# The gate sums of the last pair of experts held in their own PSUM bank across a conditional part, with the silu behind it

## The chip, the core and the metric

The kernel runs on one core of a Trainium2 chip. The time is the device time of one execution in microseconds (us); the median of three runs of the kernel before is 784.7 us. The engines have streams of their own and meet at semaphores: TensorE (PE, its weight loads PEld), VectorE (DVE), ScalarE (ACT), GpSimd (POOL) and the queue that issues most DMAs (SP).

## What is computed

A trunk of two layers over 256 tokens of width 1024. Each layer has a mixer and then a mixture of experts; the change is in the experts alone.

```python
def grouped_moe(h, router_w, router_bias, w_gate, w_up, w_down):
    ...                                  # router: two of 16 experts for each token
    y = jnp.zeros_like(hf)
    for e in range(N_EXPERTS):           # 16 experts, 1024 -> 512 -> 1024
        act = jax.nn.silu(hf @ w_gate[e]) * (hf @ w_up[e])
        y = y + combine[:, e:e + 1].astype(hf.dtype) * (act @ w_down[e])
    return y.reshape(bsz, s_len, d)

def reference(...):
    for l in range(DEPTH):               # DEPTH = 2
        ...
        x = x + g1 * mix
        h = rmsnorm(x, norm_ffn[l]) * (1.0 + sc2) + sh2
        x = x + g2 * grouped_moe(h, router_w, router_bias, moe_w_gate[l], moe_w_up[l], moe_w_down[l])
    return rmsnorm(x, final_norm)
```

## The kernel before

The experts are taken in eight pairs, `pr` 0 to 7. For a pair, up to 64 tokens (`CAP`) of each of its two experts are gathered into `xg` (once for two pairs), multiplied with the gate weights (`up(..., "g")`, tile `g`, 32 matmuls in the trace) and with the up weights (tile `u`, 32), and `act` is silu(g) times u. `actT` transposes it, `down` multiplies with the down weights (tile `dn`, 32), `evicted` and `high_low` scale the result and split it in two parts (`ys`), and `scatter` adds it to the accumulators `acc`, which hold their four banks for the whole stage. The work of a pair overlaps that of the next: while pair `pr` has its gate sums made, the result of `pr - 1` or `pr - 2` is being scaled and scattered.

Weights come in pieces of 1 MB, 12 for a pair, into a ring of 16 buffers; SP issues them in the order in which they are used, each as soon as its buffer was read for the last time. In layer 0 the last down piece of pair 7 is issued by POOL (line 1518, `following`), behind a one-element copy (line 1590, tile `cs`) that reads the first down piece of that pair and so starts when that one has landed.

Short-lived sums take turns in three PSUM banks (`bank`, tag `ps`, `bufs=3`): a request gets the bank that was given out longest ago and waits until what was in it has been read. `bankx` is one more bank, for transposes.

If an expert has more than 64 tokens, `rest` (lines 1396 to 1434) does the pairs' remaining tokens. It is code that is skipped when no count exceeds 64; with these inputs the branch to its end is taken on every engine, in both layers. `rest` is written in the middle of pair 7: behind the gate sums and the scatter of pair 5 (lines 1509, 1510), ahead of `down` of pair 6 and the up sums of pair 7. What is waited for across the skipped part works by counts: each engine that jumps over it adds, at the place it jumps to, what its skipped instructions would have added to its own semaphore (`EVENT_SEMAPHORE` on line 1398), and an instruction behind the branch that needs a bank which the skipped part would have used waits for that count. The engines take the branch independently, each when its own stream gets there.

Line 1512, ahead of `rest`, takes the silu of pair 7's gate sums from their bank to SBUF (`sg`), since `rest` would use the three banks:

```python
            if pr == 7:
                for h in range(2):
                    scattered(h)
                sg = live.tile([128, 512], F32, tag="sq", name=f"sg{l}_7", bufs=2)
                S.activation(sg, gb_, AF.Silu)
                ...
                rest(quad, top=top, ...)
                ...
                late = scales(6, down(6, iter(w6), at), old)
```

## Time and profile before

| | us |
|---|---|
| median of three runs (784.68 to 785.6) | 784.7 |
| the profiled execution | 782.88 |
| its span, first to last instruction | 781.2 |
| TensorE matmuls busy | 717.0 |
| VectorE busy | 314.9 |
| ScalarE busy | 235.0 |

The trace is of one execution; what it does not cover is 1.7 us around the span. Times in the trace count from the start of the span. The experts of layer 0 run from about 200 to 420 us, those of layer 1 from about 553 us to the end.

In a timeline row the first number is the start, the second how long the row's instructions took together, and the bracket the idle time of the engine ahead of it and what ended that. An engine's name with a q is its sequencer: it branches, waits and issues DMAs while the engine itself is idle or still works. `ACTq L1398` is ScalarE's sequencer at the branch of `rest`.

### The profile page before, as it was taken

The numbers are of one execution on the slowest core, as the hardware profiler recorded it, in microseconds if no ns is written. First come the engines' busy times: TensorE is split into PE (matmuls) and PEld (weight loads), VectorE is DVE, ScalarE is ACT, GpSimd is POOL, SyncE is SP. The second block draws the span as 40 slices with busy tenths as digits, with TensorE's granted clock in tenths as the row PEclk, the third lists the DMA queues.
The fourth block names the chain that finished last, engine by engine and source line by source line (L and its number), as shares of the span: only waits on it lengthen the run. The fifth ranks groups of instructions, "written<-read, shape, count | busy, mean of one in ns | idle before, by whom it ended". The sixth has DMA issues, their size and how long they took to land. (4 is left out here: it accounts for less than half of the span.)

```text
span 781.2 us, 10574 instructions
## 1 busy us (share of the span) xinstructions
PE 717.0 (92%) x4121; PEld 393.3 (50%) x4121; DVE 314.9 (40%) x567; ACT 235.0 (30%) x441; POOL 120.8 (15%) x168
## 2 busy tenths in 40 slices
PE   6798878998999999999798999999899999999985
PEld 4398643676434445343233777579434334434323
DVE  4459979566213113121114745454513123213214
ACT  3457667544102001110112535552402001001012
POOL 2357658022000000000004500010300000000000
PEclk9999999998999999999999899999999999999999
DMA  9999769964999999999999999496799999999993
GB/s 358 385 372 420 312 231 362 374 227 159 350 411 409 410 409 409 409 409 409 409 404 371 396 412 349 173 404 251 291 393 410 409 409 409 409 409 409 410 403 108
DMA packets 74712, 282.45 MB, mean 362 GB/s; under 512 B 5194, under 2 KB 6438, under 8 KB 69530
## 3 DMA queue, kind: packets, MB, share of 16 engines
q1 hardware_dynamic: 73122, 278.68, 90.7%
q0 software_dynamic: 1344, 2.64, 1.0%
q8 instruction: 34, 0.56, 0.3%
q10 hardware_dynamic: 184, 0.34, 0.1%
q14 instruction: 28, 0.23, 0.1%
HBM read 280.59 MB, written 1.05 MB: 361 GB/s over the span
## 5 line engine op out<-in xcount | busy, mean ns | idle before, releaser
L1267 PE MATMUL g<-w,xg 128*64 128x512 f32 x512 | 114.8, 596 | 2.8 <-DMA w<-in_moe_w_gate_dram 1.8
L1267 PE MATMUL u<-w,xg 128*64 128x512 f32 x496 | 110.7, 594 | 2.5 <-DMA w<-in_moe_w_up_dram 2.5
L1300 PE MATMUL dn<-w,at 128*64 128x512 f32 x448 | 101.7, 604 | 7.7 <-ACTq L1398 6.5
L1279 DVE TENSOR_TENSOR act<-sg,u 128x512 f32<-128x512 f32 (+1 forms) x18 | 11.1, 628 | 153.7 <-PE u L1267 153.7
L1267 PEld LDWEIGHTS u<-w,xg 128*64 128x64 f32 x496 | 34.5, 137 | 72.5 <-issue 64.1
L1267 PEld LDWEIGHTS g<-w,xg 128*64 128x64 f32 x512 | 34.9, 137 | 69.4 <-issue 60.9
L429 PE MATMUL pj<-hT,g 128*128 128x256 f32 x480 | 61.7, 286 | 5.7 <-DVE g L56 4.5
L1300 PEld LDWEIGHTS dn<-w,at 128*64 128x64 f32 x448 | 31.2, 138 | 70.4 <-issue 56.8
L56 DVE TENSOR_TENSOR g<-wi,g 128x512 fp32r<-128x512 f32 x72 | 57.0, 801 | 23.7 <-ACT g L55 22.4
L429 PEld LDWEIGHTS pj<-hT,g 128*128 128x128 f32 x480 | 58.1, 189 | 9.8 <-DVE g L56 6.6
L459 PE MATMUL po<-cat,g 128*128 128x256 f32 x372 | 52.9, 296 | 3.9 <-ACT gsr L1021 1.7
L55 ACT ACTIVATE g<-wi 128x512 fp32r<-128x512 f32 x72 | 44.5, 626 | 38.0 <-PE pj L429 20.6
L424 PE MATMUL pj<-g,hT 128*128 128x512 f32 x192 | 51.2, 419 | 5.1 <-ACT hT L350 3.1
L190 PE MATMUL ada<-ad,cond 128*32 128x512 f32 x384 | 50.1, 630 | 4.9 <-DMA ad<-in_ada_w_dram 4.9
L459 PEld LDWEIGHTS po<-cat,g 128*128 128x128 f32 x372 | 48.1, 201 | 9.3 <-issue 2.7
L424 PEld LDWEIGHTS pj<-g,hT 128*128 128x128 f32 x192 | 36.7, 198 | 19.1 <-DVE g L56 4.2
L565 DVE SCALAR_TENSOR_TENSOR yc<-yp,epar,yc 128x256 f32<-128x256 f32 x56 | 41.4, 754 | 2.3 <-POOL yc L580 1.7
L580 POOL TENSOR_TENSOR yc<-yc,cv 128x256 f32<-128x256 f32 x45 | 39.2, 872 | 19.7 <-ACT cv L579 12.0
L1332 ACT ACTIVATE ys<-y 128x512 fp32r<-128x512 f32 x28 | 16.9, 625 | 66.8 <-DVE y L1322 62.0
L1290 DVE COPY at<-at 128x512 f32<-128x512 f32 x14 | 9.7, 692 | 67.2 <-PE at L1289 67.2
L1326 ACT ACTIVATE y<-dn,cw 128x512 f32<-128x512 f32 x7 | 4.8, 687 | 104.1 <-PE dn L1300 104.1
L1275 ACT ACTIVATE sg<-g 128x512 f32<-128x512 f32 x14 | 8.4, 597 | 89.3 <-PE g L1267 89.3
(381 smaller groups left out, 859.6 us busy)
## 6 DMA issues: line engine op xcount, KB each, us to landing
w<-in_moe_w_gate_dram SPq DMA_DIRECT2D x64, 1024.0 KB, 17.2
w<-in_moe_w_up_dram SPq DMA_DIRECT2D x62, 1024.0 KB, 18.3
w<-in_moe_w_down_dram SPq DMA_DIRECT2D x61, 1024.0 KB, 18.1
ad<-in_ada_w_dram SPq DMA_DIRECT2D x48, 1024.0 KB, 8.3
wi<-in_w_in_even_dram SPq DMA_DIRECT2D x20, 512.0 KB, 12.3
wi<-in_w_in_odd_dram SPq DMA_DIRECT2D x14, 512.0 KB, 12.5
wo<-in_w_out_even_dram SPq DMA_DIRECT2D x4, 1024.0 KB
wo<-in_w_out_odd_dram SPq DMA_DIRECT2D x4, 1024.0 KB, 18.7
```

The costliest lines, as they stand in the source:

```text
L55: S.activation(g[0], w, AF.Copy)
L56: (eng or V).tensor_tensor(g[1], w, g[0].bitcast(F32), op=OP.subtract)
L190: PE.matmul(acc[32 * j:32 * j + 32, :], lhsT=cond[:, k, :], rhs=w[:, k - (i if n == 2 else 2 * i), c0:c0 + 512], start=i == 0, stop=i == 4 ...
L424: PE.matmul(bs[t], lhsT=self.h[j][:, k, t * 128:(t + 1) * 128], rhs=g[i], start=k == 0 and p == 0, stop=k == 7 and p == 2)
L429: PE.matmul(bs[c // 2][:, (c % 2) * T:(c % 2 + 1) * T], lhsT=g[i][:, c * 128:(c + 1) * 128], rhs=self.h[j][:, k, :], start=k == 0 and c % ...
L459: PE.matmul(self.acc[kd // 2][:, (kd % 2) * T:(kd % 2 + 1) * T], lhsT=block(g[wi], kd % 4), rhs=cats[ci][:, k, :], start=start and kd % 2 ...
L565: V.scalar_tensor_tensor(yc[:, k], yp[:, k, j:j + T], epar[:, k, j:j + 1], yc[:, k], op0=OP.mult, op1=OP.add)
L580: G.tensor_tensor(y, y, p, op=OP.add)
L1267: PE.matmul(b[64 * e:64 * e + 64, :], lhsT=xg[:, k, o + 64 * e:o + 64 * e + 64], rhs=we[:, e, k % 2 * 512:k % 2 * 512 + 512], start=k == 0 ...
L1279: V.tensor_tensor(a[:, n], sg[:, n], ub[:, n], op=OP.mult)
L1300: PE.matmul(bs[h][64 * e:64 * e + 64, :], lhsT=at[k][:, 64 * e:64 * e + 64], rhs=r[:, e], start=k == 0, stop=k == 3)
L1332: S.activation(ys[:, 0, n], y[h], AF.Copy)
```

## The change

`bank` gets a turn counter. Two requests of three get one of two banks under the tag `ps`, the third the one bank under a tag of its own, `pq`. Requests made inside `rest` (`two=True`) use the two `ps` banks only and don't advance the counter. The counter is set to 1 at pair 6 of each layer, so that the gate sums of pair 7 fall on `pq`; they stay there across `rest`, and the silu is written behind it. Because the counter is set, requests later in the program may fall on another of the three banks than before.

```diff
-    def bank(name):
-        return psum.tile([128, 512], F32, tag="ps", name=name)
+    turn = [0]
+
+    def bank(name, two=False):
+        tag, bufs = ("ps", 2) if two or turn[0] % 3 < 2 else ("pq", 1)
+        turn[0] += not two
+        return psum.tile([128, 512], F32, tag=tag, name=name, bufs=bufs)
...
             def all(self, q, s=0):
                 self.onehot(q, s)
                 self.weighted(q)
-                self.gather(q, s)
+                self.gather(q, s, two=True)
...
-                                b = bank(f"o{l}_{pr}_{s}")
+                                b = bank(f"o{l}_{pr}_{s}", True)
...
-                                b = bank(f"o{l}_{pr}_{s}{h}")
+                                b = bank(f"o{l}_{pr}_{s}{h}", True)
...
             if pr == 6:
+                turn[0] = 1
...
                 for h in range(2):
                     scattered(h)
-                sg = live.tile([128, 512], F32, tag="sq", name=f"sg{l}_7", bufs=2)
-                S.activation(sg, gb_, AF.Silu)
 
                 w6, w, w7 = ([*ws] for ws in (weights(6, 8, 12), w, weights(7, 8, 12 if l else 11)))
                 rest(quad, top=top, spare=live.tile([128, 8 * T], F32, tag=("h", "xT")[l], name=f"spare{l}", bufs=(2, 1)[l])
                      .rearrange("p (i n) -> p i n", i=4))
                 if following:
                     w7.append(following(w7[0], lambda: weight(7, 11, eng=G)))
+
+                sg = live.tile([128, 512], F32, tag="sq", name=f"sg{l}_7", bufs=2)
+                S.activation(sg, gb_, AF.Silu)
                 late = scales(6, down(6, iter(w6), at), old)
```

(`gather` and `gathers` hand `two` on to `bank`.) No engine has an instruction more or less that works on data; line numbers behind `bank` are 5 to 7 higher after the change. Three places show what moved.

ScalarE in layer 0, before, at the end of the code ahead of the branch (`sg_6` and `sg_7` are the silus of pairs 6 and 7, `y_5` and `ys_5` the scaled and split result of pair 5, `COMPARE_AND_BRANCH` the branch of `rest`):

```order
L1275 ACTIVATE sg_6_0_2839<-g_6_0_2789 128x512 [waits DVE_49,PE_49]
L1326 ACTIVATE y_5_00_2885<-dn_5_00_2859,cw_2_2385 128x512 [waits DVE_49,PE_49]
L1332 ACTIVATE ys_5_0_2896<-y_5_00_2885 128x512 [waits Activation_49]
L1332 ACTIVATE ys_5_0_2896<-y_5_01_2894 128x512 [waits DVE_49]
L1512 ACTIVATE sg_7_2942<-g_7_0_2901 128x512 [waits PE_49]
L1398 COMPARE_AND_BRANCH
```

The same stretch after the change:

```order
L1280 ACTIVATE sg_6_0_2839<-g_6_0_2789 128x512 [waits DVE_49,PE_49]
L1331 ACTIVATE y_5_00_2885<-dn_5_00_2859,cw_2_2385 128x512 [waits DVE_49,PE_49]
L1337 ACTIVATE ys_5_0_2896<-y_5_00_2885 128x512 [waits Activation_49]
L1337 ACTIVATE ys_5_0_2896<-y_5_01_2894 128x512 [waits DVE_49]
L1403 COMPARE_AND_BRANCH
```

ScalarE behind the branch, after the change (the branch leads to the `UNCONDITIONAL_BRANCH` that waits; `y_6` and `ys_6` are the scaled and split result of pair 6):

```order
L1403 UNCONDITIONAL_BRANCH [waits Activation_49,Activation_sequencer_49]
L1525 ACTIVATE sg_7_7748<-g_7_0_2901 128x512 [waits PE_49]
L1331 ACTIVATE y_6_00_7768<-dn_6_00_7750,cw_3_2667 128x512 [waits DVE_49,PE_49,Activation_49]
L1337 ACTIVATE ys_6_0_7772<-y_6_00_7768 128x512 [waits Activation_49]
L1337 ACTIVATE ys_6_0_7772<-y_6_01_7770 128x512 [waits DVE_49]
```

The silu, which waits for TensorE's gate sums, went from ahead of ScalarE's branch to the first place behind it; nothing else on ScalarE moved, in either layer.

TensorE in layer 0 behind the branch, before (`dn_6` are the down sums of pair 6 with their four pieces of weights `w_6_8` to `w_6_11`, `u_7` the up sums of pair 7; rows without a wait between them are left out):

```order
L1398 UNCONDITIONAL_BRANCH [waits PE_49,PE_sequencer_49]
L1300 MATMUL dn_6_00_7750<-w_6_8_2944,at_6_2887 64x512 [waits DVE_49,DMAHW2_49,PE_49,Activation_49]
L1300 MATMUL dn_6_01_7751<-w_6_8_2944,at_6_2887 64x512 [waits DVE_49,Activation_49]
L1300 MATMUL dn_6_00_7750<-w_6_9_2946,at_6_2887 64x512 [waits DMAHW3_49]
L1300 MATMUL dn_6_00_7750<-w_6_11_2950,at_6_2887 64x512 [waits DMAHW5_49]
L1267 MATMUL u_7_0_7777<-w_7_4_2952,xg_3_2665 64x512 [waits DMAHW6_49]
```

and after:

```order
L1403 UNCONDITIONAL_BRANCH [waits PE_49,PE_sequencer_49]
L1305 MATMUL dn_6_00_7750<-w_6_8_2942,at_6_2887 64x512 [waits DVE_49,DMAHW2_49,PE_49,Activation_49]
L1305 MATMUL dn_6_01_7751<-w_6_8_2942,at_6_2887 64x512 [waits DVE_49,PE_49,Activation_49]
L1305 MATMUL dn_6_00_7750<-w_6_9_2944,at_6_2887 64x512 [waits DMAHW3_49]
L1305 MATMUL dn_6_00_7750<-w_6_11_2948,at_6_2887 64x512 [waits DMAHW5_49]
L1272 MATMUL u_7_0_7777<-w_7_4_2950,xg_3_2665 64x512 [waits DMAHW6_49,Activation_49]
```

The down sums still wait for a count of ScalarE that its jump adds; the up sums now wait for ScalarE too, for the silu that empties `pq`.

TensorE in the mixer of layer 1, before (four groups of pooling sums `py`, ahead of them the sums `alow`):

```order
L853 MATMUL alow<-hT_7970,walow 32x256 x8
L858 MATMUL py_8129<-ppt_8091,inpw 128x256 [waits DMASW1_49,Activation_49]
L858 MATMUL py_8134<-ppt_8097,inpw 128x256 [waits Activation_49]
L858 MATMUL py_8137<-ppt_8103,inpw 128x256 [waits DVE_49]
L858 MATMUL py_8140<-ppt_8109,inpw 128x256 [waits DVE_49]
L190 MATMUL ada_7900<-ad_8147,cond 32x512 [waits DMAHW3_49]
```

and after:

```order
L858 MATMUL alow<-hT_7970,walow 32x256 x8
L863 MATMUL py_8129<-ppt_8091,inpw 128x256 [waits DMASW1_49,Activation_49]
L863 MATMUL py_8134<-ppt_8097,inpw 128x256 [waits Activation_49]
L863 MATMUL py_8137<-ppt_8103,inpw 128x256 [waits DVE_49]
L863 MATMUL py_8140<-ppt_8109,inpw 128x256
L195 MATMUL ada_7900<-ad_8147,cond 32x512 [waits DMAHW3_49]
```

No row moved, but the banks were dealt out in another turn. Before, the third `py` waited until VectorE had read the first one's bank, and the fourth until VectorE had copied `alow` out of its bank; after, it is the third that gets the bank of `alow` and waits for that copy, and the fourth waits for nothing more.

## Rows read from the trace of the kernel before

**Rows 1.** Chain that ended last, first pieces: start, us, what

```profile
746.08 0.04 issue
746.12 7.09 PE dn L1300 x32
```

**Rows 2.** Timeline of layer 1 around the branch

```profile
735.27 0.64 ACT L1332 ACTIVATE ys<-y 128x512 fp32r<-128x512 f32 x1 [1.34 <-DVE y L1322]
...
740.79 2.14 PE L1356 MATMUL acc<-ys,pt 128*128 128x512 f32 x8
740.91 0.60 ACT L1512 ACTIVATE sg<-g 128x512 f32<-128x512 f32 x1 [5.01 <-PE g L1267]
...
746.12 7.09 PE L1300 MATMUL dn<-w,at 128*64 128x512 f32 x32 [3.19 <-ACTq L1398]
```

**Rows 3.** Sequencers at the branch, both layers: count, ns min/median/max, first and last start

```profile
L1398 DVEq EVENT_SEMAPHORE  x4: 21/21/21, 384.8 to 741.6; - x4
L1398 PEldq EVENT_SEMAPHORE  x4: 51/51/51, 388.9 to 743.1; - x4
L1398 ACTq EVENT_SEMAPHORE  x4: 17/17/17, 392.0 to 746.1; - x4
...
L1398 DVEq COMPARE_BRANCH  x2: 74/82/90, 379.1 to 735.9; - x2
L1398 PEldq COMPARE_BRANCH  x2: 355/371/387, 386.6 to 738.1; - x2
L1398 ACTq COMPARE_BRANCH  x2: 54/61/68, 386.7 to 740.9; - x2
```

**Rows 4.** TensorE's own waits of line 1300 behind the branch, layer 0

```profile
L1300 PEldq EVENT_SEMAPHORE  x2: 51/51/51, 389.2 to 389.3; - x2
```

**Rows 5.** The same waits in layer 1

```profile
L1300 PEldq EVENT_SEMAPHORE  x2: 51/51/51, 743.3 to 743.4; - x2
```

**Rows 6.** Timeline of layer 0 around the branch

```profile
378.45 0.63 ACT L1332 ACTIVATE ys<-y 128x512 fp32r<-128x512 f32 x1 [1.47 <-DVE y L1324]
...
386.60 2.21 PE L1350 MATMUL acc<-pt,ys 128*128 128x256 f32 x16
386.72 0.60 ACT L1512 ACTIVATE sg<-g 128x512 f32<-128x512 f32 x1 [7.64 <-PE g L1267]
...
392.09 8.78 PE L1300 MATMUL dn<-w,at 128*64 128x512 f32 x32 [3.28 <-ACTq L1398]
```

**Rows 7.** Timeline of layer 0, to the last down piece

```profile
409.23 0.19 POOL L1590 COPY cs<-w 128x1 f32<-128x1 f32 x1 [197.38 <-SPq L1398]
409.87 0.81 POOL L1251 DMA_DIRECT2D w<-in_moe_w_down_dram  x1 [0.46 <-issue]
...
416.82 1.94 PE L1300 MATMUL dn<-w,at_7arow 128*64 128x512 f32 x8 [0.48 <-DMA w<-in_moe_w_down_dram]
```

**Rows 8.** Stretches of TensorE: start:end, us, busy (x), granted clock, DMA share, GB/s

```profile
575.00:740.00 165.00, 165.00 (x820) 1.00 1.03 409
392.60:396.10 3.50, 3.50 (x12) 0.51 1.03 407
```

**Rows 9.** SP's last weight DMA in the timeline

```profile
757.90 1.24 SPq L1248 DMA_DIRECT2D w<-in_moe_w_down_dram  x1
```

**Rows 10.** The same DMA among the issues: KB, us to landing

```profile
w<-in_moe_w_down_dram SPq DMA_DIRECT2D x1, 256.0 KB, 8.8
```

**Rows 11.** TensorE's last matmuls of line 1300

```profile
L1300 PE MATMUL dn<-w,at_7arow x6: 379/379/379, 769.5 to 770.0; 128*64 128x256 f32 x6
```

**Rows 12.** Timeline of the pooling sums in the mixer of layer 1

```profile
451.44 1.92 PE L858 MATMUL py<-ppt,inpw 128*128 128x256 f32 x6 [0.47 <-ACT ppt L846]
452.18 0.42 DVE L862 COPY alowT<-alow 128x256 f32<-128x256 f32 x1 [0.63 <-PE py L858]
...
452.66 0.30 PEld L858 LDWEIGHTS py<-ppt,inpw 128*128 128x128 f32 x2 [0.49 <-DVE alowT L862]
453.29 0.16 PEld L190 LDWEIGHTS ada<-ad,cond 128*32 128x32 f32 x8 [0.33 <-issue]
```

## Prediction

> **What bounds the kernel now.** I read the chain that ended last first. It begins at 746.08 us, at the branch of `rest` in layer 1, and TensorE's down sums of pair 6 are its next piece [rows 1]: from there to the end everything follows on TensorE and then on the final scaling, so what starts those down sums sooner ends the kernel sooner. The timeline there shows TensorE idle for 3.19 us ahead of them, until ScalarE's sequencer at line 1398 let go [rows 2]; layer 0 has the same hole, 3.28 us [rows 6].

> The view of the sequencers tells why ScalarE is the last. Each engine branches when its stream gets there and reports from the other side later: VectorE branches at 379.1 and 735.9 and reports from 384.8 and 741.5 (the last of its four counts starts at 741.6), 5.6 us later; ScalarE branches at 386.7 and 740.9 and reports at 392.0 and 746.1, 5.2 to 5.3 us later [rows 3]. The branch itself takes ScalarE 54 to 68 ns, so the rest of the 5.2 us lies between it and the code behind it. ScalarE comes late because the silu stands ahead of its branch and waits for the gate sums: idle for 7.64 us in layer 0 and 5.01 in layer 1 [rows 2, 6]. TensorE's own reports start at 388.9 and about 743.0 (the second of the pair at 743.1) [rows 3], right as its scatter of pair 5 is done: 386.60 + 2.21 = 388.81 and 740.79 + 2.14 = 742.93 [rows 2, 6].

> **The change, part by part.** *The silu behind the branch.* It removes nothing and adds no work: two silus of 0.60 us [rows 2, 6] change place. ScalarE's last instruction ahead of the branch is now the split of pair 5's result, which starts at 378.45 and 735.27 [rows 2, 6]. Sequencers run ahead of their engines by one instruction here (the branch at 740.9 goes with a silu that starts at 740.91), so ScalarE branches at about 378.5 and 735.3. With its 5.3 us it reports at 383.8 and 740.6; with VectorE's 5.6 us, and branching only when the split has ended, at 384.7 and 741.5. Either is ahead of TensorE's own report.

> What is late next is TensorE itself: report, then its remaining waits for the first down sums, which start at 389.2 and 389.3 in layer 0 and at 743.3 and 743.4 in layer 1, 0.05 us each [rows 4, 5]. Counting from the last wait's start with its 0.05 and as much for the first weight load, the down sums can start at 389.4 and 743.5. Before they started at 392.09 and 746.12 [rows 2, 6]: 2.7 us sooner in layer 0, 2.6 in layer 1. VectorE's report, 1.4 us and more ahead of TensorE's, holds nothing up.

> *What the silu's new place could hold up.* Behind it on ScalarE stands the scaling of pair 6, which needs the down sums. The new wait is that of the up sums of pair 7 for the bank `pq`: the silu still starts when the gate sums are done, at 386.7 and 740.9, and is over 0.6 us later [rows 2, 6], while the up sums come 32 down matmuls, 7.09 us [rows 2], behind the branch. Cost nothing; if the silu's start were tied to ScalarE's report it would still be over by 742.1.

> *Layer 0, what becomes of 2.7 us.* Nothing, I think. The last down piece of pair 7 is issued by POOL at 409.87, behind a copy at 409.23 that waits for another piece's landing, and TensorE stands idle 0.48 us for it before it goes on at 416.82 [rows 7]. That issue hangs on transfers alone, so it stays where it is; TensorE comes up to 2.7 us sooner and waits that much longer. Bounds 0 to 2.7; I take 0, since the wait is there already.

> *Layer 1.* TensorE is busy for all of the 165 us from 575 to 740, at full clock, beside a DMA share of 1.03 [rows 8]. Behind it the weights must be there sooner. SP's last DMA is issued at 757.90 and lands 8.8 us later, at 766.7 [rows 9, 10]. Its four matmuls are the last of the six that start from 769.5 to 770.0 [rows 11], so they start at about 769.7; their waits may stand one pair of matmuls, 0.2 us, ahead. That leaves 2.8 us, 0.2 more than needed. So 2.6 us counts in full, at most 2.8.

> *The banks' new turn.* In the mixer of layer 1 the third `py` now waits for the copy of `alow`, which ends at 452.60. Before, only the fourth did; it starts its loads at 452.66, and the loads for `ada` follow at 453.29 [rows 12], 0.63 us on. After, the third starts where the fourth did, and the fourth and `ada` move back by the third's time: at least 0, if a later wait absorbs it, at most those 0.63 us. I take 0.4: in the 0.63 us are 0.33 us that the row calls issue [rows 12], part of which will overlap. TensorE is nearly always busy in this stretch, so I count it.

> *Sum.* The profiled execution is 782.88: 782.88 - 2.6 + 0.4 = 780.7. It stands 1.8 us below the median of the runs, 784.7; the same difference there gives 784.7 - 2.2 = **782.5 us**, 0.28% less. From both terms' ends: 784.7 - 2.8 = 781.9 to 784.7 - 2.6 + 0.6 = 782.7.

> [...]

> **The rivals.** *Serial jumps (slower).* VectorE and ScalarE now branch within 0.7 us of each other. If what the 5.2 us go for is served one engine at a time, ScalarE would begin when VectorE is through: in layer 1 at 741.5 + 5.3 = 746.8, after the 746.1 of before, 0.7 us lost; the hole is then 3.9 us, and after the 3.28 us of layer 0 the granted clock fell to 0.51 [rows 8], the lower of its two levels, and the same 32 matmuls took 8.78 instead of 7.09 us [rows 2, 6]: 1.7 more. With the 0.4 of the banks: 784.7 + 0.7 + 1.7 + 0.4 = 787.5. It decides from a jump of 10.2 us (746.1 - 735.9). Against it: in layer 1 VectorE's and TensorE's jumps ran together from 738.1 to 741.5, and VectorE's 5.6 us were the same in layer 0, where it jumped alone. Chance 4 in 100. [...]

> *The weights bind the end of layer 1.* TensorE and the transfers are nearly tied there, with 0.2 us left. In runs in which the last landing is 1 to 2.8 us later against TensorE's work, the gain shrinks by 0.8 to all of it: 783.3 to 785.1. For it: a DMA share of 1.03 over the whole stage. Against: the landing goes by issue times that the change does not touch, and a TensorE that is 0.4 us later at the start of the stage widens the room. Chance 15 in 100, at about 784.1.

> *More than the sum.* The hole of layer 1 is nearly as long as that of layer 0, and in the runs that were timed it may often cost the clock too, 1.7 us, which a hole of 0.5 us would not: 780.8, chance 10 in 100. Layer 0's 2.7 us could pass if the last piece came earlier: 779.8, 5 in 100.

> *It doesn't do what it says.* Something else that TensorE waits for comes at the same time as ScalarE's report and keeps the hole: 785.1. The rows name only ScalarE, twice. 4 in 100.

> **How the numbers follow.** The forecast, 782.5, has 62 in 100. The range 780.5 to 784.4 leaves out the serial jumps, the change without effect, layer 0's gain and the later part of the weights' case, some 20 in 100. A measurement of this kernel can tell about 0.2%, 1.6 us, from no change: faster means below 783.1. That holds for the forecast but for a few in 100 (0.6 us of banks and a little less gain), and for the two cases of more: 0.74. Slower means above 786.3: 0.04. The rest, 0.22, is the same.

> **What the profile would show.** Right: ScalarE's branches near 378.5 and 735.3, its reports before 385 and 742; the silu behind them, still at the end of the gate sums; TensorE's idle time ahead of the down sums of pair 6 about 0.6 us in both layers; in layer 0 more waits of TensorE for weights behind the branch and the last down piece again near 416.8; in layer 1 the chain shorter by 2.6 us with the last down matmuls close behind the last landing; the third `py` on `alowT`. Wrong: a ScalarE report later than TensorE's, waits for down weights at 764 to 768 us, or a layer 0 that ends more than 0.5 us away from where it does.

## The result and the profile after

Beside fresh runs of the kernel before, the changed kernel takes 780.34 us (median of 15 runs, 779.22 to 783.76) against 784.7 (median of 15, 782.52 to 787.36). The ratio is 0.9949, 95% interval 0.9933 to 0.9965: 4.0 us less, between 2.7 and 5.3. Forecast were 782.5 us and 2.2 us less. The direction was right; the median lies 0.16 us under the low end of the range, by the ratio (784.7 x 0.9949 = 780.7) just inside it, and the size is what the experiments are about.

The profiled execution takes 781.72 us, its span is 780.0 (before 781.2). What the prediction looked for is in its trace. First the chain that ended last, its first pieces (start, us, what), which answers to [rows 1]:

```profile
744.62 0.30 issue
744.92 7.09 PE dn L1305 x32
```

Layer 1 around the branch in the timeline, which answers to [rows 2]:

```profile
736.70 0.63 ACT L1337 ACTIVATE ys<-y 128x512 fp32r<-128x512 f32 x1 [1.34 <-DVE y L1327]
...
742.23 2.14 PE L1361 MATMUL acc<-ys,pt 128*128 128x512 f32 x8
742.35 0.60 ACT L1525 ACTIVATE sg<-g 128x512 f32<-128x512 f32 x1 [5.01 <-PE g L1272]
...
744.92 7.09 PE L1305 MATMUL dn<-w,at 128*64 128x512 f32 x32 [0.56 <-PEq L1403]
```

The silu still starts when the gate sums are done, but the down sums of pair 6 no longer wait for ScalarE's sequencer: they start 0.55 us behind the scatter's end (742.23 + 2.14 = 744.37), after 3.19 us before [rows 2], and what ends the rest of the hole is TensorE's own sequencer (PEq). The sequencers at the branch, now line 1403, in both layers (count, ns min/median/max, first and last start; answers to [rows 3]):

```profile
L1403 ACTq EVENT_SEMAPHORE  x4: 17/17/17, 385.5 to 742.0; - x4
L1403 DVEq EVENT_SEMAPHORE  x4: 21/21/21, 386.5 to 743.1; - x4
L1403 PEldq EVENT_SEMAPHORE  x4: 51/51/51, 390.6 to 744.6; - x4
L1403 POOLq COMPARE_BRANCH  x2: 54/54/54, 222.4 to 577.6; - x2
L1403 POOLq EVENT_SEMAPHORE  x2: 17/17/17, 222.6 to 577.8; - x2
L1403 ACTq COMPARE_BRANCH  x2: 54/61/68, 380.2 to 736.7; - x2
L1403 DVEq COMPARE_BRANCH  x2: 74/82/90, 380.8 to 737.4; - x2
```

ScalarE branches with the start of its last split (736.70) and reports 5.3 us later in layer 0 and 5.2 in layer 1 (the first of the pair at 741.9), VectorE 5.7 and 5.6 us after its own branch. Both are ahead of TensorE, whose reports come last. ScalarE's and VectorE's jumps now run side by side, 0.6 to 0.7 us apart, and each takes what it took alone: the rival of serial jumps is out.

Layer 0, to the end of its down sums, which answers to [rows 6, 7]:

```profile
388.31 2.20 PE L1355 MATMUL acc<-pt,ys 128*128 128x256 f32 x16
388.42 0.60 ACT L1525 ACTIVATE sg<-g 128x512 f32<-128x512 f32 x1 [7.62 <-PE g L1272]
...
391.14 5.37 PE L1305 MATMUL dn<-w,at 128*64 128x512 f32 x24 [0.63 <-PEq L1403]
...
396.95 1.94 PE L1305 MATMUL dn<-w,at 128*64 128x512 f32 x8 [0.44 <-DMA w<-in_moe_w_down_dram]
...
417.74 1.94 PE L1305 MATMUL dn<-w,at_7arow 128*64 128x512 f32 x8 [0.88 <-DMA w<-in_moe_w_down_dram]
```

The hole is as short as in layer 1, the clock does not fall (24 matmuls in 5.37 us, 0.22 each, at a granted clock of 1.00), and then TensorE waits for weights: already within pair 6's down sums, and 0.88 us for the last piece, 0.48 before [rows 7].

The mixer of layer 1, which answers to [rows 12]:

```profile
452.35 0.70 PE L863 MATMUL py<-ppt,inpw 128*128 128x256 f32 x2 [0.47 <-ACT ppt L851]
453.08 0.42 DVE L867 COPY alowT<-alow 128x256 f32<-128x256 f32 x1 [0.63 <-PE py L863]
...
453.56 1.13 PE L863 MATMUL py<-ppt,inpw 128*128 128x256 f32 x4 [0.52 <-DVE alowT L867]
454.62 1.06 PE L195 MATMUL ada<-ad,cond 128*32 128x512 f32 x8
```

The third `py` waits for `alowT`, as forecast, and `ada` starts 2.27 us behind the second `py`; before, 453.29 - 451.44 = 1.85 [rows 12]. That is 0.42 us.

So both terms are there with their size, and yet the profiled executions differ by 1.2 us in span and the medians by 4.4. To the end of layer 1's last down sums the two timelines add up so: -2.62 us in layer 1, +0.43 for the banks, -0.80 in layer 0 (29.96 to 29.16 us, in the second table below), +1.66 ahead of the experts of layer 0 and +0.11 ahead of those of layer 1, which makes -1.2. The third was forecast at nothing; more traces, below, tell what it is. The fourth is visible in the stretch ahead of the experts (start:end, us, TensorE busy, granted clock, DMA share, GB/s), before and after:

```profile
0.00:200.00 200.00, 167.10 (x1138) 0.97 0.84 322
```

```profile
0.00:200.00 200.00, 168.78 (x1130) 0.95 0.83 319
```

The first gate sums of layer 0 start at 198.34 before and at 200.00 after. Nothing of the change lies ahead of them; in this execution the granted clock was 0.95 over this stretch, before it was 0.97. What the medians differ by cannot be read from one pair of executions.

### The profile page after: what moved, and what is told of

It is laid out like the page before. It is cut to its first block, busy times and chain, and to the rows that moved or that the text cites. A ratio compares the mean times of both kernels' runs of the same rounds, so it can differ in the third digit from the quotient of the medians.

```text
span 780.0 us, 10577 instructions
## 1 busy us (share of the span) xinstructions
PE 720.2 (92%) x4121; PEld 395.7 (51%) x4121; DVE 315.1 (40%) x567; ACT 235.0 (30%) x441; POOL 120.8 (15%) x168
```

## The experiments

Three views were tested. **Theory A**: layer 1's hole is the gain, layer 0's is swallowed by the wait for weights, the banks cost 0.43 us; what was measured beyond this is scatter or the clock behind the hole of layer 1. **Rival B**: layer 0's 2.7 us reach the end in the timed runs. **Rivals C and D**: the clock behind the holes, or other stretches, carry a good part.

All runs, beside runs of the kernel before on the same chip (median, ratio with its interval, the ratio times 784 us):

| kernel | us | ratio | us against before |
|---|---|---|---|
| changed | 780.34 | 0.9949 [0.9933, 0.9965] | -4.0 |
| changed, second time | 781.26 | 0.9963 [0.9947, 0.9979] | -2.9 |
| changed, third time | 781.27 | 0.9970 [0.9949, 0.9991] | -2.4 |
| silu moved in layer 1 only | 782.71 | 0.9974 [0.9945, 1.0003] | -2.0 |
| the same, second time | 781.07 | 0.9966 [0.9948, 0.9984] | -2.7 |
| silu moved in layer 0 only | 783.58 | 0.9986 [0.9961, 1.0011] | -1.1 |
| banks alone | 785.52 | 1.0018 [0.9987, 1.0049] | +1.4 |
| before against itself | 782.48 | 0.9985 [0.9957, 1.0012] | -1.2 |
| changed, `py` banks as before | 780.62 | 0.9953 [0.9936, 0.9970] | -3.7 |
| before, layer 1's hole filled, 12 matmuls | 791.7 | 1.0100 [1.0076, 1.0123] | +7.8 |
| before, both holes filled, 12 matmuls | 798.08 | 1.0184 [1.0159, 1.0210] | +14.4 |
| before, layer 1's hole filled, 6 matmuls | 783.21 | 0.9996 [0.9979, 1.0014] | -0.3 |
| before, both holes filled, 6 matmuls | 783.47 | 0.9996 [0.9978, 1.0015] | -0.3 |

And from the timelines of the profiled executions, in us: the start of layer 0's first gate sums; from the end of the scatter behind which the hole is to the end of the last down sums, in layer 0 and in layer 1; from the start of `alow` to that of `ada`; from there to layer 1's first gate sums.

| kernel | first gate sums | layer 0 | `alow` to `ada` | to layer 1 | layer 1 |
|---|---|---|---|---|---|
| before | 198.34 | 29.96 | 4.88 | 103.88 | 27.40 |
| before against itself | 196.61 | 29.82 | 4.88 | 104.29 | 27.49 |
| banks alone | 197.08 | 29.91 | 5.31 | 103.88 | 29.25 |
| layer 0 only | 198.43 | 29.98 | 5.31 | 105.92 | 27.48 |
| layer 1 only | 200.00 | 29.43 | 5.31 | 105.77 | 24.79 |
| layer 1 only, second | 197.43 | 29.97 | 5.31 | 104.01 | 24.85 |
| changed | 200.00 | 29.16 | 5.31 | 103.99 | 24.78 |
| changed, second | 198.82 | 30.05 | 5.31 | 105.91 | 24.85 |
| changed, third | 198.49 | 29.74 | 5.31 | 103.90 | 25.07 |
| `py` banks as before | 198.09 | 29.93 | 4.88 | 103.88 | 24.78 |
| layer 1 filled, 6 | 195.79 | 29.93 | 4.88 | 104.31 | 27.48 |
| both filled, 6 | 197.14 | 29.94 | 4.88 | 104.11 | 27.52 |

The column from `alow` to `ada` repeats to the hundredth. Layer 1 takes 24.8 to 25.1 us with the silu behind the branch and 27.4 to 27.5 with it ahead, with one exception that is told below. Layer 0 lies between 29.2 and 30.1 us, wherever the silu stands. The two columns that the change does not touch, the first and the one ahead of layer 1, wander by 4.2 and 2.0 us from one execution to the next. The two kernels with 12 matmuls are told in the text.

### One part alone: banks, layer 1, layer 0

In all three the gate sums of pair 7 are on `pq`, as in the changed kernel; what differs is where the silu is written. Banks alone:

```diff
+                sg = live.tile([128, 512], F32, tag="sq", name=f"sg{l}_7", bufs=2)
+                S.activation(sg, gb_, AF.Silu)
                 rest(quad, ...)
-                sg = live.tile([128, 512], F32, tag="sq", name=f"sg{l}_7", bufs=2)
-                S.activation(sg, gb_, AF.Silu)
```

> The changed kernel with the silu written ahead of the conditional part again; the banks keep their new turn. The theory of the prediction (term sizes: layer 1 -2.6 us, layer 0 nothing, banks +0.4): the time of before plus 0.4, within 0.2% of it; TensorE idle 3.2 us ahead of pair 6's down sums in both layers, the third py on alowT. Rival A (the new turn itself gains what the measured result has beyond the sum, some 1.8 us): 1.8 us below before. Rival B (layer 0's 2.7 us pass) and rival C (the holes cost the clock in the timed runs) expect the same here as the theory: before plus 0.4, with a mean granted clock like that of before.

Layer 1 only (layer 0 only has the two conditions exchanged):

```diff
+                if l == 0:
+                    sg = ...; S.activation(sg, gb_, AF.Silu)
                 rest(quad, ...)
+                if l == 1:
                     sg = ...; S.activation(sg, gb_, AF.Silu)
```

> The changed kernel with the silu behind the conditional part in layer 1 alone; in layer 0 it stands ahead of it as before. Theory: before minus 2.6 plus 0.4 = minus 2.2 us, and the same time as the full change. Rival B (layer 0's 2.7 us pass in the timed runs): the full change is faster than this one by 1 to 2.7 us. Rival C (the half-clock stretch behind a hole of 3.2 us costs about 1.7 us in many runs, and the hole of 0.6 us does not): minus 2.2 minus up to 1.7 = up to 3.9 us below before, with a mean granted clock higher than that of before by up to 0.002.

> The changed kernel with the silu behind the conditional part in layer 0 alone; in layer 1 it stands ahead of it as before. Theory: before plus 0.4 (the banks), since the last down piece of layer 0 still lands when it did: TensorE's last down matmuls of layer 0 start within 0.5 us of where they did, counted from the first DMA-bound piece of pair 7. Rival B: 0.6 to 2.3 us below before, with that start as much sooner. Rival C: the time of before or a little below, if the half-clock stretch behind the hole of layer 0, 3.4 us long, is what layer 0's slack does not hide.

Measured: +1.4, -2.0 and -1.1 us, with intervals some 2 us to either side. These tell one thing: banks alone lies no more than 1.0 us below before, so its rival A, that the new turn gains 1.8 us, is out. For the others they are too wide. Set beside each other, layer 0 only is 2.0 us faster than banks alone on the mean of the runs (0.3 to 3.7), as rival B would have it; a later pair, below, has it the other way. The traces tell more. Moving the silu in layer 1 takes layer 1 from 27.4 to 24.8 us; moving it in layer 0 leaves layer 0 at 30.0 us: TensorE starts the down sums 0.56 us behind the scatter and then waits for weights. Down sums of pair 6 and the last piece in layer 0, silu moved there:

```profile
389.74 3.65 PE L1305 MATMUL dn<-w,at 128*64 128x512 f32 x16 [0.56 <-PEq L1403]
...
417.23 1.94 PE L1305 MATMUL dn<-w,at_7arow 128*64 128x512 f32 x8 [1.23 <-DMA w<-in_moe_w_down_dram]
```

The same in banks alone, where the hole of layer 0 is there and the granted clock falls behind it, to 0.50 from 391.7 to 394.9 us:

```profile
390.89 8.78 PE L1305 MATMUL dn<-w,at 128*64 128x512 f32 x32 [3.23 <-ACTq L1403]
...
415.64 1.94 PE L1305 MATMUL dn<-w,at_7arow 128*64 128x512 f32 x8 [0.49 <-DMA w<-in_moe_w_down_dram]
```

The one waits for pieces of weights from pair 6's down sums on, 0.7 us more at the last one alone; the other loses 2.7 us to the hole and 1.7 to the clock, and both need 29.9 to 30.0 us in all.

Banks alone has one more thing, in layer 1 (timeline, and the granted clock of a part of it, columns as above):

```profile
745.53 8.78 PE L1305 MATMUL dn<-w,at 128*64 128x512 f32 x32 [3.36 <-ACTq L1403]
```

```profile
746.60:749.90 3.30, 3.30 (x12) 0.50 1.03 408
```

Here the granted clock did fall behind layer 1's hole too, to 0.50, and the 1.7 us are not swallowed: layer 1 takes 29.25 us. That is the prediction's rival of more than the sum, seen in one of the four traces in which TensorE idles in that hole.

### The kernel before against itself

> The kernel before, unchanged, against itself, to have the mean granted clock of each of its timed runs beside the span. All theories: ratio 1. Theory (the excess of the measured gain over 2.2 us is the scatter of short half-clock stretches): at the same mean granted clock the spans of before lie 2.2 us above those of the changed kernel (778.9 us at a clock of 0.981). Rival C: the clocks of before are lower as a rule by 0.002 (one stretch of 3.4 us at half clock more in 780). Rival B: the clocks are alike and the spans are 4 us apart.

Ratio 0.9985, interval 0.9957 to 1.0012: the same program differs from itself by 1.2 us here, so a difference of that size between two sets of runs has to be read with its interval. Its granted clocks, 0.972 to 0.981, overlap with those of the changed kernel, 0.974 to 0.985; at 0.981 its spans are 779.8 to 783.6 us, those of the changed kernel 778.6 and 779.6. That spread at one clock was expected by none of the theories, and it is too wide to test the 2.2 us.

### The changed kernel again, and with layer 1 alone beside it

The changed kernel was run two more times without an edit, the second time beside layer 1 only on the same chip.

> The changed kernel, unchanged, beside the next three. Terms as the traces have them so far: layer 1's hole -2.7 us, layer 0 nothing, banks +0.43, so -2.3 us for an execution without half-clock stretches of its own. Theory A (behind the hole of layer 1 the clock halves in part of the runs, 1.7 us each time, and layer 0's gain is swallowed): 2.3 to 4.0 us below before. Rival B (layer 0's move is worth another 2 us, as the means of the runs with and without it so far suggest): 4 to 4.5 us below before. Rival C (the first comparison was off by the scatter of before): 2.3 us below before or less.

> The changed kernel beside the next one, for the question what layer 0's move is worth. Theory A (layer 0's gain is swallowed): 2.3 to 3 us below before, and within 0.5 us of the next kernel but for the scatter. Rival B (layer 0's move is worth some 2 us in the timed runs): 4 us below before and 2 us below the next kernel.

> The silu behind the conditional part in layer 1 alone, as in layer1_only, on the same chip as the changed kernel. Theory A: the time of the changed kernel within 0.5 us, 2.3 to 3 us below before; in the trace the time from the scatter's end to the end of layer 0's last down sums is 29.8 us in both. Rival B: 2 us above the changed kernel, with a mean granted clock lower by 0.004 as in the earlier runs.

Measured: -2.9, -2.4 and -2.7 us. Rival B expected 2 us between the last two; they differ by 0.3 us, the other way. Their traces in layer 0, first layer 1 only, then the changed kernel:

```profile
392.31 7.09 PE L1305 MATMUL dn<-w,at 128*64 128x512 f32 x32 [3.25 <-ACTq L1403]
...
417.09 1.94 PE L1305 MATMUL dn<-w,at_7arow 128*64 128x512 f32 x8 [0.26 <-DMA w<-in_moe_w_down_dram]
```

```profile
389.17 3.65 PE L1305 MATMUL dn<-w,at 128*64 128x512 f32 x16 [0.63 <-PEq L1403]
...
416.35 1.94 PE L1305 MATMUL dn<-w,at_7arow 128*64 128x512 f32 x8 [0.86 <-DMA w<-in_moe_w_down_dram]
```

The down sums start 2.6 us sooner behind the scatter (2.83 after its start at 386.34, against 5.46 after 386.85), the last piece 0.2 (30.01 and 30.24 us after those starts). Over all traces without the large filling, layer 0 takes 29.84 us on the mean with the silu ahead of the branch (six traces of the second table without the filled hole of layer 0) and 29.77 with it behind (five). The traces of either group lie up to 0.5 and 0.9 us apart, so this tells 0.07 us from 2.7 and not from a few tenths, and the 0.80 us of the first pair are within it. In the traces, layer 0's gain is swallowed.

Rival B's other sign did come. The mean granted clock of the timed runs is 0.979 to 0.981 in the six kernels and repetitions whose layer 0 has no hole, and 0.976 to 0.979 in the others on record (the kernels with 12 matmuls left out). A higher clock is not yet less time, though: with both holes filled (below) it is 0.979, with layer 1's alone 0.977, and both take the same time.

### The banks as before

```diff
+        t0 = turn[0]
         b = bank("alow")
...
+            turn[0] = t0 + (1, 2, 1, 0)[g]
             pb = bank(f"py{g}")
...
+        turn[0] = t0 + 5
```

The third `py` gets the bank of the first, the fourth that of `alow`, as in the kernel before.

> The changed kernel with the four py sums and alow given the banks in the order that they had before: the third py gets the bank of the first, the fourth that of alow. The theory of the prediction: the stretch from alow to ada takes 4.88 us in the trace, as before, and not 5.31; time 0.43 us below the changed kernel, 2.7 below before plus what theory A adds. Rival D (the new turn costs 1.3 us or more, as the means of the runs of banks_alone suggest, and not in this stretch): the stretch is 4.88 and the time 0.4 below the changed kernel, with another 0.9 lost in other stretches that are longer than before in the trace; by that rival the other stretches differ from before by more than the half-clock stretches explain.

The stretch, in the timeline:

```profile
452.31 1.92 PE L865 MATMUL py<-ppt,inpw 128*128 128x256 f32 x6 [0.47 <-ACT ppt L851]
453.05 0.42 DVE L869 COPY alowT<-alow 128x256 f32<-128x256 f32 x1 [0.63 <-PE py L865]
...
454.15 1.07 PE L195 MATMUL ada<-ad,cond 128*32 128x512 f32 x8
```

From `alow` to `ada` it is 4.88 us, as before, and 5.31 in every kernel with the new turn: the term is 0.43 us. No other stretch of the second table is longer than before by more than it wanders, so rival D has nothing in the traces. In the timed runs it is not out: banks alone, +1.4 us, and this kernel, by the table 0.8 us faster than the changed one beside it, both lie on its side of 0.43, and both intervals hold 0.43 too. The time is 3.7 us below before, interval 2.4 to 5.0. This version has both gains in its trace and is ahead of the kernel before; that it beats the changed one is shown by that stretch of the trace alone, since 0.4 us is below what the runs tell apart.

### The hole filled

The kernel before with useless matmuls behind the branch, so that TensorE is busy while ScalarE's report is awaited; the silu and the banks stay. First 12 on one half of the array:

```diff
                 rest(quad, ...)
...
+                if l == 1:
+                    dm = bankx(f"dm{l}")
+                    for i in range(12):
+                        PE.matmul(dm[0:64, :], lhsT=at[i % 4][:, 0:64], rhs=w6[0][:, i % 2, 0:512],
+                                  start=i == 0, stop=i == 11)
```

> The kernel before with 12 useless matmuls of 128x512 (2.66 us by 0.22 each) on TensorE right behind the conditional part of layer 1, ahead of pair 6's down sums: the silu and the banks stay as before, pair 6's down sums still wait for ScalarE's report, but TensorE is busy meanwhile. Theory A: no half-clock stretch behind the hole, so 0.4 to 1.7 us below before on the mean, and never the slower; the down sums start 3.2 us behind the scatter's end as before. Rival B and C: the time of before. A cost of its own, if the last useless matmul ends behind the report: up to 0.3 us.

> As the last, in both layers. Theory A: the time of that one, since the half clock behind layer 0's hole lies ahead of a wait for weights and costs nothing; in the trace no half-clock stretch behind the branch of layer 0 and the same time from the scatter's end to the end of layer 0, 29.9 us. Rival B in the form that the clock is what layer 0's move gives back: 2 us below the last one, with a mean granted clock higher by 0.002 to 0.004. Rival B in the form that the earlier start passes: the time of the last one.

They missed, by my sizing: I had taken 12 rows of 0.22 us, and there were twice as many, each twice as long. Layer 1 with 12 matmuls, 24 rows in the trace (23 below and one at 753.90):

```profile
744.01 10.06 PE L1522 MATMUL dm<-w,at 128*64 128x512 f32 x23 [0.45 <-PEq L1398]
753.48 0.64 PE L1300 MATMUL dn<-w,at 128*64 128x512 f32 x1
```

A row of the down sums, which are written in pairs on the two halves of the array, costs 0.22 us (7.09 / 32); on one half alone it is 0.44 (10.06 / 23), and the pairs below bring the same matmuls to 0.23 (2.79 / 12). The down sums came 9.92 us behind the scatter instead of 3.2. The kernel was 7.8 us slower, and with layer 0 filled too another 6.6: there the down sums came 6.5 us later than with layer 1 alone filled (9.92 and 3.43 us behind the scatter), and layer 0 took 34.97 instead of 29.59 us. So layer 0 swallows what comes sooner, but not what comes 6.5 us later: 5.4 us of that passed.

Then 6 matmuls in pairs, `dm[64 * e:64 * e + 64, :]` with `e = i % 2`, for the same place:

> The kernel before with 6 useless matmuls in the hole of layer 1, this time in pairs on the two halves of the array as pair 6's down sums are, 12 rows of 0.22 us or 2.66 us in all; in the earlier kernel 12 of them without pairs took 10 us and delayed what follows. Theory A (part of the gain of the change is that the clock no longer halves behind the hole): the down sums start 3.2 us behind the scatter's end as before, then 24.2 us to the last down sums in every trace, and a mean 0.4 to 1 us below before. Rival C (the hole's clock is nothing): the time of before. Cost of its own at most 0.2 us.

> As the last, in both layers. Theory A: the time of that one within the scatter; in the trace no half-clock stretch behind layer 0's branch, and the same 29.8 us from the scatter's end to the end of layer 0's last down sums, so that a half-clock stretch there is shown to cost nothing; the mean granted clock 0.980 against 0.977 of before. Rival B in the form that the clock is what layer 0's move gives back: 1.5 to 2 us below the last one.

Layer 1 with 6 matmuls:

```profile
740.24 2.14 PE L1356 MATMUL acc<-ys,pt 128*128 128x512 f32 x8
742.90 2.79 PE L1523 MATMUL dm<-w,at 128*64 128x512 f32 x12 [0.52 <-PEq L1398]
745.64 7.09 PE L1300 MATMUL dn<-w,at 128*64 128x512 f32 x32
```

The hole is full, the down sums start 3.26 us behind the scatter as before. Both kernels take the time of before, 0.3 us less with 1.4 us to either side. What the idle hole does to the clock is therefore not the whole of what the change gains: it is at most 1.7 us by these intervals. That it is less is likely and not shown. In layer 0 of the second of these two pair 6's down sums take 7.09 us, in the first, where the hole is open, 8.78, and layer 0 takes 29.94 and 29.93 us: the 1.7 us there cost nothing.

## Why the prediction was right, and where it was off

**The silu behind the branch** was right in each step. ScalarE branches with the start of the split, reports 5.2 to 5.3 us later, ahead of TensorE, and TensorE's own report and waits are what is late next; I had the down sums 0.6 us behind the scatter's end, they are 0.55 to 0.63 in all traces with the silu behind. The silu's new place holds nothing up. In layer 0 the timeline names ScalarE's split of pair 6 for 0.72 us of idle TensorE ahead of the up sums of pair 7, but in layer 1 the same up sums start at 751.81, ahead of that split at 752.10, so they do not need it; in layer 0 a wait for their weights fits the times, since TensorE starts on a piece every 2.6 us there (396.95, 399.61, 402.20).

**Layer 1's 2.6 us** came in full: 27.40 to 24.78 us in the first pair of traces, 24.78 to 25.07 over all six. The room ahead of the last weights, 0.2 us by my sum, was enough in five of the six. Where layer 1 takes 25.07 us (the changed kernel, third time), the last down sums are slower than in the first, which has 3.61 in their place:

```profile
764.14 3.83 PE L1305 MATMUL dn<-w,at_7arow 128*64 128x512 f32 x24
```

In the same execution, the list of what the engines idled for ahead of line 1305 from 755 to 770 us (us, times) has this entry:

```profile
  DMA w<-in_moe_w_down_dram: 0.8, 2
```

The trace of the first has no such entry there. So the rival of the weights was real, but small: it took 0.2 to 0.3 us once in six traces, where I had 0.8 us and more.

**Layer 0's swallowed 2.7 us**: right in the traces, 29.84 against 29.77 us. The mark that I gave for wrong, a layer 0 that ends more than 0.5 us away from where it did, came true in the first trace: its last down sums end at 419.68 us, before at 418.76. It was a bad mark. The whole stage starts at another time in each execution, and counted from the scatter single traces still lie up to 0.9 us apart; only the means can be compared.

**The banks** cost 0.43 us where I took 0.4.

**The sum**, -2.6 + 0.4 = -2.2, is what the traces show of its two terms: -2.62 + 0.43 = -2.2 for the first pair. The weak step is the last, the range: "784.7 - 2.8 = 781.9 to 784.7 - 2.6 + 0.6 = 782.7" and the low end 780.5 were worked out from the ends of the terms and from one rival, with nothing for the scatter of the medians on which they were set. The three medians of the changed kernel lie 0.9 us apart (780.34 to 781.27), those of before in four comparisons, the three of the experiments and the first, 1.1 us (783.64 to 784.7), and the difference that was measured went from 4.0 to 2.9 and 2.4 us for the same two programs. The base of 784.7 was the highest of those four medians. The first interval, 2.7 to 5.3 us, does not hold 2.2, the two others do. That the first result still lies at the edge of the range is luck: the low end had been set for the clock behind layer 1's hole, and in the first pair of traces there is nothing of it, since before ran those 32 matmuls in 7.09 us [rows 2].

**What stays open** is what the change gains beyond 2.2 us. Weighted by their intervals, the three comparisons give 3.2 us, 2.4 to 4.0 (an estimate from the first table), so a little more than the sum is likely. A half clock behind layer 1's hole (granted 0.50), 1.7 us in one trace of four, would add about 0.4, which the sum had at nothing and the prediction among its rivals; the filled hole bounds this part to 1.7 us and does not separate it from nothing. Least squares, which seek the three terms that fit all timed runs of the kernels without filling best (with one base for each chip), give layer 1 -3.0 us, layer 0 -1.3 (-2.0 to -0.6) and the banks +1.2 (0.3 to 2.1): in the timed runs layer 0 may pass on a part of its 2.7 us, which the traces do not show. All 2.7 us of it are borne out by neither.

**The length of the jump.** The branch instruction takes ScalarE 54 to 68 ns, the way to the code behind it 5.2 to 5.3 us [rows 3], before and after the change, and the sum worked out from that row came out.

## What to carry to other kernels

## What the runs showed of the hardware

The DMA queues show one thing more between a branch and its report. In layer 0 before, ScalarE branches at 386.7 and reports at 392.0 [rows 3]; VectorE 379.1 and 384.8. Packets of the queue kind `instruction` (packets, MB, share of the 16 engines) from 390.1 to 390.6 us, and from 382.7 to 383.1 (the first stretch also holds one of another queue, `q8`):

```profile
q14 instruction: 1, 0.01, 4.0%
```

```profile
q14 instruction: 1, 0.01, 5.2%
```

In the changed kernel, with the branches of ScalarE and VectorE at 380.2 and 380.8, from 383.2 to 385.2:

```profile
q1 hardware_dynamic: 210, 0.79, 100.8%
q14 instruction: 2, 0.02, 2.1%
```

Each of these jumps has one packet on `q14` ahead of its report, 3.4 to 4.0 us behind the branch and 1.4 to 2.1 us ahead of the report by the ends of these two stretches, and it moves in about 0.3 us (5.2% of 16 engines in 0.4 us) while the queue `q1` with the weights fills the engines. GpSimd, whose branch is 0.2 us from the code behind it, has no such packet. TensorE's jump in layer 0 took no more than 2.3 us, from 386.6 to 388.9 [rows 3], so 5.2 us is not the length of every jump. What the packet carries, and whether the report waits for it, the traces do not show; the packets of ScalarE's and VectorE's jumps stand under one number, `q14`. Whether the jump is shorter when no weights are moving was not tried. Nor was what the kernel's own hint for this branch does: it is given for TensorE, VectorE, ScalarE and SP, and GpSimd, which has none, is the one with the short jump.

The clock behind a hole is not the same each time. Behind 3.2 to 3.4 us of idle TensorE in layer 0 pair 6's down sums took 8.65 to 8.78 us in five of seven traces and 7.09 in the two others, at the same waits; in layer 1 they took 8.78 in one of four. The granted clock over the first 3.2 to 3.5 us of the long ones is 0.51 in the kernel before (layer 0) and 0.50 in banks alone (both layers). Behind 0.6 us it was not seen, in eleven places; in the changed kernel the granted clock is 1.00 there, in both layers.
